# Retention and output projection of a hybrid RWKV and retention block: four raw value buffers, four split weight buffers, constants and gates loaded behind the first fourteen loads

## The chip, the core and the metric

The kernel runs on one core of one Trainium2 chip. The core has a matrix engine (PE, whose weight loads are listed apart as PEld), a vector engine (DVE), a scalar engine (ACT), a general engine (POOL) and an engine that issues most of the DMA transfers (SP). Each engine works through its own list of instructions in a fixed order; an instruction that waits for a semaphore holds up everything behind it on its engine, and a DMA that waits holds up the DMAs behind it in the queue of the engine that issues it. The metric is the device time of one execution in microseconds (us). Before the change, three runs gave 2503.66 to 2504.76 us, with a median of 2504.42 us.

## The reference

One layer mixes 1024 latent tokens, behind 256 context tokens, in two branches: a bidirectional RWKV scan, and a bidirectional retention with 4 heads, keys and queries 256 wide, values 512 wide, in chunks of 128 tokens. The change touches the retention and the pools that the output projections use. For one direction the retention is:

```
def step(S, inp):
    kc, vc = inp[0], inp[1]
    S_new = S * c_dec + jnp.einsum('bhck,bhcv->bhkv', kc * k_dec, vc)
    if not with_out:
        return S_new, None
    qc = inp[2]
    scores = jnp.einsum('bhik,bhjk->bhij', qc, kc) * intra
    o = (jnp.einsum('bhij,bhjv->bhiv', scores, vc)
         + jnp.einsum('bhik,bhkv->bhiv', qc * q_dec, S))
    return S_new, o
```

`intra`, `q_dec`, `k_dec` and `c_dec` are exponentials of a per-head decay times token distances. Forward and backward outputs are added, normalised per head, multiplied by a gate and projected. The RWKV branch ends in the same way. Both projections are merged by channel gates, and a last projection and an RMSNorm follow.

## The kernel before

**Arithmetic.** Large products are done in three passes: an operand is split into a rounded part `hi` (a cast on ACT, line 210) and a rest `lo` (a subtraction on DVE or POOL, line 211), and PE adds hi x hi, hi x lo and lo x hi. The helper is `split`.

**Stages.** Up to about 1795 us of the trace the kernel computes the input projections and the RWKV scans. Then `phase2` opens: `retention` runs the four heads, and `out_a` follows, which normalises the RWKV output (`rwkv_norm`) and multiplies it by the weights `wa` (products `ya`). The scheduler interleaves the two, so `ya` products run while the retention goes on. `phase3` does, for each half of 512 tokens, the retention's projection (weights `wr`, products `yr`, 8 blocks of 4 weight groups each), the merge with the channel gates, and the last projection (weights `wo`, products `po`, lines 1541 to 1556).

**One head** (`ret_head`). The state of the backward direction is built over the chunks 1, 0, 9, 8, down to 3. For each pair of chunks: `ret_load` brings the keys (tile `rs`, 256 KB), PE transposes them (`ktp`, line 1395), ACT scales them (`kx`, line 1399) and DVE computes the rest of the split (line 1400). For each chunk `ret_vals` brings the values (tile `vr`, 256 KB, line 1380) and splits them into `vt` (ACT line 210, POOL line 211; DVE for the very first two chunks). `ret_state` multiplies both (`st`, lines 1414 to 1416), and DVE adds the result to the decayed old state (line 1429). Then chunks 2 to 9 give outputs: scores `sc`, the states times the decayed queries (`ro`, line 1475, the queries scaled by POOL in line 1408), the scores times the values (into the same `ro`), and `ret_norm`: statistics, normalised tile `on`, the gate tile `gr` (loaded in line 1497), four transposes `ot`, ACT's scale and bias, POOL's product with `gr` (line 1506), and the store (line 1507). `ret_decay` makes the decays of a head from two constant tiles, `dist` (256 KB) and `io` (128 KB), that are loaded once, for head 0 (lines 1456 and 1457).

**Buffers.** A tile of a tag gets the next of that tag's buffers and waits until its last reader is done. Lines 41 and 42 set their numbers. `VR` counts the raw values (tag `vr`): a load into a `vr` buffer waits for the POOL subtraction of the value that held it. `VT` counts the split values, `RS` keys and queries. `WR` counts raw weights, and `WH` the tiles `hi` and `lo`, which `weights` uses for `wa`, `wr` and `wo`, and `rwkv_norm` for its sums. In `ya` and `yr` each split weight serves 12 matmuls in a row. In `po`, eight weights are used in two groups of four; within a group four token tiles each use all four weights, 48 matmuls in all, so that all four stay in use until the last tile of the group.

**Order.** A scheduler places the instructions on each engine. Two helpers tie it down: `lead` remembers an instruction under a letter, and `late` forbids an instruction to stand ahead of the one remembered. `load` (line 573) issues a DMA on SP that may not stand ahead of the lead "s". `first` (line 1354) makes each of the retention's first `FIRSTL` = 14 loads the lead "s" in turn; these are the keys and values of head 0 for the chunks 1, 0 and 9 to 3 (the last of them is the value of chunk 3). A plain `nc.sync.dma_start` is not tied in this way. In the DMA queues, each new transfer also waits until the transfer eight before it has landed.

Of the kernel before, what the change touches and what calls it, by code (L numbers as in the profile page):

```python
# [15 lines left out]
P = 128  # L16
# [21 lines left out]
XB = 14  # L38
EARLY = 6
LAG = 2  # L40
VR, VT, RS, KX, S1, S0, ON = 2, 11, 6, 3, 9, 2, 2
WR, WH, AR = 3, 5, 2
RES = 4
MUE = 1
VAE = 0
# [83 lines left out]
class Kern:  # L129
# [1303 lines left out]
    def ret_head(self, h, dist, io):  # L1433
        nc = self.nc
# [18 lines left out]
            if c > 2:  # L1453
                sb[c - 1] = self.ret_state(h, 1, k1, vt, c, sb[c])
        if h == 0:
            nc.sync.dma_start(dist.rearrange("p a b -> p (a b)"), self.ins["k_dist"])
            nc.sync.dma_start(io.rearrange("p a b -> p (a b)"), self.ins["k_iota"])
        qd, mk = self.ret_decay(h, dist, io)
        for c in range(2, 10):
            if c % 2 == 0:  # L1460
# [24 lines left out]
    def ret_norm(self, h, t0, po):  # L1485
        nc, pv = self.nc, self.pv
        on = self.rt("on", [P, 512], ON)
        st = self.rt("bst", [P, 6], 4)
        nc.vector.bn_stats(st, po)
        mv = self.rt("bmv", [P, 4], 4)  # L1490
        nc.vector.bn_aggr(mv[:, 0:2], st)
        nc.scalar.activation(mv[:, 2:3], mv[:, 1:2], AF.Ln, bias=self.eps[:, 2:3])
        nc.scalar.activation(mv[:, 2:3], mv[:, 2:3], AF.Exp, scale=-0.5)
        nc.vector.tensor_scalar(on, po, mv[:, 0:1], mv[:, 2:3], op0=ALU.subtract, op1=ALU.mult)
        yield
        gr = self.rt("gr", [P, 4, P], 2)
        nc.sync.dma_start(gr, self.grD[4 * h:4 * h + 4].rearrange("v p t -> p v t")[:, :, t0:t0 + P])
        pt = self.rpsum("ot", (P, 4, P))
        for v in range(4):
            nc.tensor.transpose(pt[:, v, :], on[:, P * v:P * v + P], self.ident)  # L1500
        y = on.rearrange("p (v t) -> p v t", v=4)
        for v in range(4):
            b = 4 * h + v
            nc.scalar.activation(y[:, v, :], pt[:, v, :], AF.Identity, scale=self.ph[:, PV_RLW + b:PV_RLW + b + 1],
                                 bias=self.ph[:, PV_RLB + b:PV_RLB + b + 1])
        nc.gpsimd.tensor_tensor(y, y, gr, op=ALU.mult)
        nc.sync.dma_start(self.orD[4 * h:4 * h + 4].rearrange("v p t -> p v t")[:, :, t0:t0 + P], y)
        yield
# [87 lines left out]
```

## Time and profile before

The profiled execution took 2498.37 us, of which the trace spans 2496.6 us; the runs' median of 2504.42 us is 6.05 us above it. In the table, the columns are windows of the trace (us), the busy time of PE, DVE and ACT within them, and the mean rate of the transfers.

| window | what runs | length | PE | DVE | ACT | GB/s |
|---|---|---|---|---|---|---|
| 0 to 1795 | input projections, RWKV | 1795.00 | 1722.90 | 1212.90 | 853.81 | 144 |
| 1795 to 2200 | retention, `ya` | 405.00 | 380.54 | 283.22 | 205.31 | 185 |
| 2200 to 2496.6 | rest of `yr`, merge, `po` | 296.60 | 282.54 | 153.10 | 102.97 | 173 |

The profile gives for each group of instructions the line, engine, operation and tiles, written out<-in. In timelines each row has its start, its duration, and in brackets the time for which its engine had been idle, with what ended the wait. "SPq" is SP's queue of DMAs. The granted clock (PEclk) is the share of TensorE's full speed that the throttle let through. PE fills 96% of the whole span.

### The profile page before, as it was taken

The numbers are of one execution on the slowest core, as the hardware profiler recorded it, in microseconds if no ns is written. First come the engines' busy times: TensorE is split into PE (matmuls) and PEld (weight loads), VectorE is DVE, ScalarE is ACT, GpSimd is POOL, SyncE is SP. The second block draws the span as 40 slices with busy tenths as digits, with TensorE's granted clock in tenths as the row PEclk, the third lists the DMA queues.
The fourth block names the chain that finished last, engine by engine and source line by source line (L and its number), as shares of the span: only waits on it lengthen the run. The fifth ranks groups of instructions, "written<-read, shape, count | busy, mean of one in ns | idle before, by whom it ended". The sixth has DMA issues, their size and how long they took to land.

```text
span 2496.6 us, 53437 instructions
## 1 busy us (share of the span) xinstructions
PE 2386.0 (96%) x21200; PEld 1926.1 (77%) x21200; DVE 1649.2 (66%) x2882; ACT 1162.1 (47%) x2547; POOL 562.3 (23%) x688
## 2 busy tenths in 40 slices
PE   7999999999999899997999999999898998999998
PEld 4888888777888899986777777777666765678786
DVE  5497897797796254434887787884378657754644
ACT  6434334334334334444655666554356435543422
POOL 2211021211021001211222322222276335400000
PEclk9999999999999899998999999999999999999999
DMA  6143344343344625354546556554465755585552
GB/s 250 50 149 118 140 152 135 133 141 121 135 156 152 199 88 146 106 139 124 157 145 175 163 170 192 149 160 135 123 187 165 224 160 156 180 285 170 182 174 85
DMA packets 335660, 385.07 MB, mean 154 GB/s; under 512 B 86954, under 2 KB 240306, under 8 KB 331314
## 3 DMA queue, kind: packets, MB, share of 16 engines
q1 hardware_dynamic: 304370, 298.80, 39.0%
q0 software_dynamic: 10944, 55.58, 6.7%
q10 hardware_dynamic: 20096, 27.27, 3.1%
q8 instruction: 167, 2.74, 0.4%
q14 instruction: 83, 0.68, 0.1%
HBM read 264.63 MB, written 116.92 MB: 153 GB/s over the span
## 4 chain that ended last, share of the span: by engine, by line
PE 53%; DMA 5%; DVE 5%; ACT 3%; issue 2%; SPq 2%; POOL 2%; ACTq 0%; DVEq 0%; POOLq 0%
PE gm L556 10%; PE gv L556 7%; PE ro L1475 3%; PE A L556 2%; PE yr L1276 2%; PE yr L1274 2%; PE yr L1275 2%; DMA bi<-bkD 2%; PE S L556 2%; PE X L556 2%; PE bt L1043 2%; PE gm L330 2%; PE gm L332 1%; PE gm L331 1%; PE U L556 1%
## 5 line engine op out<-in xcount | busy, mean ns | idle before, releaser
L330 PE MATMUL gm<-uh,wh 128*128 128x512 f32 x896 | 354.2, 396 | 16.2 <-ACT xp L402 13.7
L331 PE MATMUL gm<-ul,wh 128*128 128x512 f32 x896 | 353.7, 395 | 0.7 <-DVE ul L299 0.7
L332 PE MATMUL gm<-uh,wl 128*128 128x512 f32 x896 | 353.2, 394 | 0.0
L330 PEld LDWEIGHTS gm<-uh,wh 128*128 128x128 f32 x896 | 169.6, 190 | 51.5 <-ACT xp L402 15.0
L1063 POOL TENSOR_TENSOR sp<-sv,pc 64x256 f32<-64x256 f32 x152 | 104.9, 690 | 424.9 <-DVE sv L1087 202.3
L331 PEld LDWEIGHTS gm<-ul,wh 128*128 128x128 f32 x896 | 169.8, 189 | 38.4 <-DVE xnt L298 1.7
L332 PEld LDWEIGHTS gm<-uh,wl 128*128 128x128 f32 x896 | 169.7, 189 | 34.9
L556 PE MATMUL gm<-uh,wlo 128*128 128x512 f32 x416 | 171.0, 411 | 0.7 <-DVE wlo L658 0.7
L556 PE MATMUL gm<-ul,whi 128*128 128x512 f32 x416 | 171.3, 412 | 0.0
L556 PE MATMUL gm<-uh,whi 128*128 128x512 f32 x416 | 170.8, 411 | 0.0
L658 DVE TENSOR_TENSOR wlo<-wraw,whi 128x256 fp32r<-128x256 f32 x168 | 81.0, 496 | 122.5 <-ACT whi L657 121.3
L556 PE MATMUL gv<-whi,uh 128*128 128x256 f32 x512 | 148.7, 290 | 0.3 <-issue 0.3
L211 DVE TENSOR_TENSOR lo<-raw,hi 128x512 fp32r<-128x512 f32 x128 | 92.3, 726 | 85.2 <-ACT hi L210 85.0
L556 PE MATMUL gv<-whi,ul 128*128 128x256 f32 x512 | 147.7, 289 | 0.0
L556 PE MATMUL gv<-wlo,uh 128*128 128x256 f32 x512 | 147.6, 288 | 0.0
L210 ACT CAST hi<-raw 128x512 fp32r<-128x512 f32 x128 | 78.6, 620 | 140.1 <-PE yr L1275 74.1
L902 DVE TENSOR_TENSOR TL<-TL,tmp 128x31 f32<-128x31 f32 (+15 forms) x310 | 135.3, 436 | 8.5
L1077 ACT COPY uv<-U 64x256 f32<-64x256 f32 x160 | 58.6, 366 | 156.3 <-PE U L556 82.7
L900 DVE TENSOR_TENSOR tmp<-E,TL 128x31 f32<-128x31 f32 (+15 forms) x310 | 124.0, 400 | 8.9
L1087 DVE TENSOR_TENSOR sv<-S,sp 64x256 f32<-64x256 f32 x144 | 60.7, 422 | 103.1 <-PE S L556 58.6
L1475 PE MATMUL ro<-s,rs 128*128 128x512 f32 x256 | 123.7, 596 | 4.8 <-DVE s L1429 4.3
L210 ACT CAST wh<-wr 128x1024 fp32r<-128x1024 f32 x56 | 58.8, 1050 | 130.7 <-PE gm L331 127.2
(298 smaller groups left out, 6228.1 us busy)
## 6 DMA issues: line engine op xcount, KB each, us to landing
wr<-in_w_in SPq DMA_DIRECT2D x56, 512.0 KB, 3.5
wraw<-in_w_in SPq DMA_DIRECT2D x84, 256.0 KB, 3.6
bkD<-bk POOLq DMA_DIRECT2D x16, 1280.0 KB, 5.6
bk<-bkD SPq DMA_DIRECT2D x80, 256.0 KB, 3.6
krD<-kr POOLq DMA_DIRECT2D x16, 1024.0 KB, 4.4
raw<-in_wr SPq DMA_DIRECT2D x64, 256.0 KB, 3.1
vtD<-vt POOLq DMA_DIRECT2D x64, 160.0 KB, 3.9
bi<-bkD SPq DMA_DIRECT2D x160, 64.0 KB, 2.6
```

Of the source, the lines that this page charges most:

```text
L210: nc.scalar.copy(hi, src)
L211: (eng or nc.vector).tensor_tensor(lo, src, hi.bitcast(F32), op=ALU.subtract)
L330: nc.tensor.matmul(acc[:, :n], hi[:, k, :], self.hi(k, t0, n), start=(k == 0), stop=False)
L331: nc.tensor.matmul(acc[:, :n], hi[:, k, :], self.lo(k, t0, n), start=False, stop=False)
L332: nc.tensor.matmul(acc[:, :n], lo[:, k, :], self.hi(k, t0, n), start=False, stop=(k == KT - 1))
L556: return self.pin(self.nc.tensor.matmul(*a, **k))
L658: self.late(nc.vector.tensor_tensor(lo[:, j % size, k:k + 2], r, h.bitcast(F32), op=ALU.subtract), "v")
L900: self.late(nc.vector.tensor_tensor(t3, et[:, j + 1:, j:j + 1].broadcast_to([P, n, m]), tl[:, j:j + 1, 0:m].broadcast_to([P, n, m]), op=AL ...
L902: self.late(nc.vector.tensor_tensor(tl[:, j + 1:, 0:m], tl[:, j + 1:, 0:m], t3, op=ALU.subtract), "v")
L1063: nc.gpsimd.tensor_tensor(sp[ch], sv[ch, h], pcs[ch].broadcast_to([64, 4, C]), op=ALU.mult)
L1087: self.lead("v", nc.vector.tensor_tensor(new[h], ps[ch], sp[ch], op=ALU.add))
L1475: nc.tensor.matmul(po, qx[d][:, k, cols], st[:, k, :], start=(d == 1 and k == 0), stop=False)
```

## The change

Raw values get four buffers in place of two. Split weights get four in place of five, for `hi` and for `lo`. The memory that the one takes is what the other gives up: a `vr` buffer holds 2 KB in each partition, and so do a `hi` and a `lo` buffer. The constants `dist` and `io`, and the gate tiles `gr` of all heads (32 loads), are issued through `load`, and so stand behind the first fourteen loads. Nothing that is computed changes.

```
-VR, VT, RS, KX, S1, S0, ON = 2, 11, 6, 3, 9, 2, 2
-WR, WH, AR = 3, 5, 2
+VR, VT, RS, KX, S1, S0, ON = 4, 11, 6, 3, 9, 2, 2
+WR, WH, AR = 3, 4, 2
...
         if h == 0:
-            nc.sync.dma_start(dist.rearrange("p a b -> p (a b)"), self.ins["k_dist"])
-            nc.sync.dma_start(io.rearrange("p a b -> p (a b)"), self.ins["k_iota"])
+            self.load(dist.rearrange("p a b -> p (a b)"), self.ins["k_dist"])
+            self.load(io.rearrange("p a b -> p (a b)"), self.ins["k_iota"])
...
         gr = self.rt("gr", [P, 4, P], 2)
-        nc.sync.dma_start(gr, self.grD[4 * h:4 * h + 4].rearrange("v p t -> p v t")[:, :, t0:t0 + P])
+        self.load(gr, self.grD[4 * h:4 * h + 4].rearrange("v p t -> p v t")[:, :, t0:t0 + P])
```

Every engine's order up to the retention stays as it was. From there on the scheduler places things anew. SP's order at the start of head 0 (a minus marks a row of before, a plus a row of the change; a row without either stands in both). `vr_21720` and `vr_21725` are the values of chunks 9 and 8, `vr_21762` and `vr_21767` those of 7 and 6, `rs` are keys and queries:

```order
 L1386 DMA rs_21718<-kD 128x2x256
+L1380 DMA vr_21720<-vD 128x512
+L1380 DMA vr_21725<-vD 128x512
 L1386 DMA rs_21760<-kD 128x2x256
 L1386 DMA rs_21802<-kD 128x2x256
 L1386 DMA rs_21844<-kD 128x2x256
-L1456 DMA dist<-in_k_dist 128x512
-L1457 DMA io<-in_k_iota 128x256
-L1380 DMA vr_21720<-vD 128x512
+L1380 DMA vr_21762<-vD 128x512
 L1386 DMA rs_21886<-kD 128x2x256
 L1386 DMA rs_21888<-qD 128x2x256
```

The values of chunks 9 and 8 have moved ahead of the keys of the later chunks. The constants have left this place; they come, with the first gates, five value loads further on.

ACT's order at the same place. `vt_21722` and `vt_21727` are the split values of chunks 9 and 8, `vt_21764`, `vt_21769` and `vt_21806` those of 7, 6 and 5, `s` are copies of first states, and `kx_21735` is the scaling of the keys of chunks 9 and 8:

```order
+L210 CAST vt_21722<-vr_21720 128x512
+L210 CAST vt_21727<-vr_21725 128x512
 L1427 COPY s_2775_21674<-st_21675 128x512
 L1427 COPY s_2775_21674<-st_21680 128x512
-L210 CAST vt_21722<-vr_21720 128x512
+L210 CAST vt_21764<-vr_21762 128x512
 L1427 COPY s_2781_21696<-st_21697 128x512
 L1427 COPY s_2781_21696<-st_21702 128x512
-L210 CAST vt_21727<-vr_21725 128x512
+L210 CAST vt_21769<-vr_21767 128x512
+L210 CAST vt_21806<-vr_21804 128x512
 L1399 ACTIVATE kx_21735<-ktp_21730,ph 128x512
```

Two casts stood ahead of the first of these key scalings, and now five do. The rows that follow on ACT go up to the key scalings of chunks 7 and 6 (`kx_21777`) and of 5 and 4 (`kx_21819`); `vt_22301` and `vt_22306` are the first two values of head 1:

```order
-L210 CAST vt_21764<-vr_21762 128x512
-L210 CAST vt_21769<-vr_21767 128x512
+L210 CAST vt_21811<-vr_21809 128x512
+L210 CAST vt_21848<-vr_21846 128x512
 L1399 ACTIVATE kx_21777<-ktp_21772,ph 128x512
-L210 CAST vt_21806<-vr_21804 128x512
-L210 CAST vt_21811<-vr_21809 128x512
+L210 CAST vt_21853<-vr_21851 128x512
+L210 CAST hi_24336<-ar_24333 128x512
+L210 CAST vt_22301<-vr_22299 128x512
+L210 CAST vt_22306<-vr_22304 128x512
 L1399 ACTIVATE kx_21819<-ktp_21814,ph 128x512
```

The casts of values run three to five chunks further ahead of the key scalings than before.

ACT's order in the first of the last projections (first half of the tokens). `hi_26420` is the fifth weight of `wo`, `hi_26429`, `hi_26438` and `hi_26447` are the sixth to eighth, and the `act` tiles are activations of the second half, loaded ahead. Before, `hi_26420` stood six rows ahead of `act_26815`; now it reads:

```order
 L210 CAST act_26810<-ar_26808 128x512
 L210 CAST act_26815<-ar_26813 128x512
+L210 CAST hi_26420<-raw_26419 128x512
 L210 CAST hi_26429<-raw_26428 128x512
 L210 CAST hi_26438<-raw_26437 128x512
-L210 CAST hi_26447<-raw_26446 128x512
 L210 CAST act_26820<-ar_26818 128x512
 L210 CAST act_26825<-ar_26823 128x512
+L210 CAST hi_26447<-raw_26446 128x512
```

The fifth weight's cast has moved behind the activation `act_26815`, next to the sixth, and the eighth's behind two further activations.

## The prediction, made before the change was run

> **What bounds the kernel now.** I begin with the head of the page.
>
> ```profile
> span 2496.6 us, 53437 instructions
> PE 2386.0 (96%) x21200; PEld 1926.1 (77%) x21200; DVE 1649.2 (66%) x2882; ACT 1162.1 (47%) x2547; POOL 562.3 (23%) x688
> ```
>
> PE is busy for 96% of the span, so only PE's gaps, and matmuls at a low clock, can be won. Next come the windows over the stages from the start of the retention to the end. The columns are: window, its length, then busy us and instructions of PE, PEld, DVE, ACT and POOL, the granted clock, the DMA share, GB/s.
>
> ```profile
> 1802.50:1808.60 6.10, 0.01 (x1) 0.01 (x1) 1.43 (x3) 2.79 (x5) 1.83 (x2) 0.78 0.90 287
> 1808.60:1826.20 17.60, 15.34 (x65) 11.66 (x65) 12.22 (x19) 8.68 (x16) 12.42 (x11) 0.88 0.62 203
> 1826.20:1882.00 55.80, 54.88 (x212) 33.70 (x212) 44.29 (x74) 33.44 (x81) 41.19 (x33) 1.00 0.62 185
> 1882.00:1912.00 30.00, 23.37 (x108) 17.63 (x109) 26.77 (x39) 17.28 (x35) 18.63 (x16) 1.00 0.44 144
> 1912.00:2080.00 168.00, 168.00 (x744) 114.74 (x743) 106.25 (x180) 73.65 (x177) 76.57 (x59) 1.00 0.61 190
> 2080.00:2120.00 40.00, 32.63 (x135) 22.41 (x134) 32.63 (x53) 22.41 (x47) 19.21 (x17) 0.96 0.45 139
> 2306.30:2352.00 45.70, 43.16 (x189) 35.07 (x188) 28.07 (x57) 21.19 (x53) 0.00 (x0) 1.00 0.50 162
> ```
>
> Where products with the output weights fill the gaps (1912 to 2080) PE has no idle time at all. What is idle lies in four places: the start of head 0 (6.09 us, then 2.26), heads 1 and 3 while they build states (6.63 and 7.37), and the first output projection (2.54). In heads 1 and 3 DVE is busy for 26.77 of 30.00 us (89%) and 32.63 of 40.00 (82%), so values that arrive earlier meet a busy DVE there. Only at the start of head 0 is it a load that PE waits for. The timelines of PE and of ACT (start, us, instruction, in brackets the idle time before it and what ended it):
>
> ```profile
> 1801.61 0.66 PE L1395 MATMUL ktp<-ident,rs 128*128 128x128 f32 x4
> 1808.59 0.79 PE L1414 MATMUL st<-vt,kx 128*128 128x512 f32 x1 [6.33 <-ACT kx L1399]
> 1809.18 0.63 PE L1415 MATMUL st<-vt,kx 128*128 128x512 f32 x1
> 1809.61 0.63 PE L1414 MATMUL st<-vt,kx 128*128 128x512 f32 x1
> 1818.33 0.50 PE L1414 MATMUL st<-vt,kx 128*128 128x512 f32 x1 [0.78 <-ACT kx L1399]
> 1826.16 1.10 PE L1475 MATMUL ro<-s,rs 128*128 128x512 f32 x2 [1.48 <-DVE s L1429]
> ```
> ```profile
> 1804.25 0.62 ACT L210 CAST vt<-vr 128x512 fp32r<-128x512 f32 x1 [4.44 <-DMA vr<-vD]
> ...
> 1807.34 0.62 ACT L210 CAST vt<-vr 128x512 fp32r<-128x512 f32 x1 [1.50 <-DMA vr<-vD]
> 1807.86 0.68 ACT L1399 ACTIVATE kx<-ktp,ph 128x512 fp32r<-128x512 f32 x1
> ```
>
> The matmul at 1808.59 waits for scaled keys, whose inputs were there at 1802.3. The scaling stood in ACT's order behind two casts of values, and the second cast waited for its load. SP issued those loads so:
>
> ```profile
> 1799.49 0.34 SPq L1456 DMA_DIRECT2D dist<-in_k_dist  x1
> 1799.87 0.54 SPq L1457 DMA_DIRECT2D io<-in_k_iota  x1
> 1800.52 0.38 SPq L1380 DMA_DIRECT2D vr<-vD  x1
> 1800.93 0.52 SPq L1386 DMA_DIRECT2D rs<-kD  x1
> 1801.56 0.56 SPq L1386 DMA_DIRECT2D rs<-qD  x1
> 1802.21 0.54 SPq L1380 DMA_DIRECT2D vr<-vD  x1
> 1802.81 0.97 SPq L1497 DMA_DIRECT2D gr<-grD  x2
> 1806.29 10.24 SPq L1380 DMA_DIRECT2D vr<-vD  x5
> ```
>
> **The front of head 0.** SP stood still before 1799.49; the first row of the next fence (what SP's queue waited for, total, times, longest) says for what. In the new order the values of chunks 9 and 8 stand ahead of that wait and have buffers of their own, so both are in the chip before 1799; the 6.33 us as they are now would go. But ACT's order changes too: the key scaling for chunk 9 now stands behind five casts, of chunks 9, 8, 7, 6 and 5. So what is late next is the load of chunk 5. Behind the wait SP now issues key, key, chunk 7, key, query, chunk 6, chunk 5: at 0.34 to 0.56 us each the seventh goes out at about 1799.49 + 6 x 0.5 = 1802.5. It ends 7 x 256 KB = 1.79 MB of transfers. Before, 1.41 MB (dist, half as much for io, chunk 9, key, query, chunk 8) had landed at 1807.34. At the 287 GB/s of the first window the further 0.38 MB take 1.3 us, which gives 1808.6; by time in flight (chunk 8: 1802.21 to 1807.31, 5.1 us by its rows on issue and cast) it is 1802.5 + 5.1 = 1807.6. I take 1808.1 + 0.52 for the cast + 0.68 for the scaling + 0.05 = 1809.4 for the first matmul, **0.8 us later** than 1808.59. The bounds: if that load flew as briefly as the shortest of its kind (2.6 us, below) it would land at 1805.1 and PE start at 1806.4, 2.2 us earlier; if the seven loads moved at the 203 GB/s of the second window, it would land at 1799.49 + 8.8 + 2.6 = 1810.9, PE start at 1812.2, 3.6 us later.
>
> ```profile
> SPq L1456 <- DMA mbD<-gp: 10.7, 1, 10.7
> SPq L573 <- POOL ar L1316: 71.2, 32, 6.9
> SPq L1380 <- POOL vt L211: 32.2, 22, 3.0
> DMA to landing us min/median/max: 2.6/3.9/6.2
> L211 POOL TENSOR_TENSOR vt<-vr,vt x38: 1262/1293/1744, 1805.0 to 2084.4; 128x512 fp32r<-128x512 f32 x38
> ```
>
> After the long gap PE runs slow: its starts lie 0.43 us apart (1809.18 to 1809.61) at a granted clock of 0.78 and 0.88 in the first two windows, against 0.226 on average where PE is full (168.00 us for 744 matmuls from 1912 on). This stays if the gap stays. The Trainium skill, "TensorE: Matmul & The Clock Gate", Part 1, says that an idle window of about 3.4 us halves PE's clock until it has been busy about as long again. The 0.43 us agree with the halving. By that rule a gap shortened under 3.4 us would also win back the slow stretch, and I use it only for the rival below.
>
> Behind 1808.59 the pace was one value for every trip of load, cast and POOL subtraction (1.29 us median), because two raw buffers went round. With four, that pace goes. Another head-of-line wait could come in its place: the scaling for chunks 5 and 4 now stands behind the casts of head 1's first two values. The later of their loads needs the buffer of chunk 4, whose subtraction ends at about 1809.4 + 0.5 + 1.29 = 1811.2; with a median flight of 3.9 us and 1.25 us for cast and scaling the keys are ready at 1816.4. PE wants them when it wanted them before and waited (1818.33 - 0.78), plus the 0.8: at 1818.4. Cover 2.0 us, just under the longest flight's excess (2.3). So what is late next there is PE's own work (15.34 of 17.60 us), then DVE's sums (12.22). Of its idle time 0.78 is waiting behind casts, and 1.48 at the first output is DVE's. I let the first go and keep the second. So the front gives +0.8 - 0.8 = **0.0**, from -3.0 (2.2 earlier and the 0.78) to +3.6.
>
> **Constants and gates.** These move behind the first 14 loads: dist and io (384 KB), and all 32 gr loads. The first reader of dist and io ahead of the outputs is the decay for the queries, whose output is wanted by POOL 12 us after PE's start (below at 1822.10). The new place in SP's order is behind the load of chunk 3, which waits for the POOL subtraction of chunk 7; by the pace of the old rows this is around 1810, and with the longest flight (6.2 us) both are there by 1817. Cover: 5 us. If it failed, first output and every later one would move by the overrun, one to one, since POOL then starts its 2.54 us late.
>
> ```profile
> 1822.10 2.54 POOL L1408 TENSOR_TENSOR rs<-rs,qd 128x512 f32<-128x512 f32 x2
> ```
>
> The first two gr loads were issued at 1802.81 and are read after the first output at 1826.16 has been normalised. They go out one and two value loads behind the constants, by about 1812; with the longest flight they are there at 1818, 8 us ahead of 1826.16. I cost them at 0.
>
> **Heads 1 to 3.** All later values run through four buffers, so the 32.2 us in which SP waited for POOL's value subtractions shrink, while the 71.2 us of waits for the RWKV norm's buffers stay; SP's order is one line, so part of the first returns in the second. In heads 1 and 3 the amount of DVE work between the first key scaling and the first score is the same but for one or two instructions, and DVE filled 89% and 82% there. Value: **0**. Ends: if a third of the idle 14.0 us went, -4.7; if the new order costs each of the two stages one more stall as long as its longest (1.76 us, next row), +3.5.
>
> ```profile
> 1890.55 0.50 PE L1414 MATMUL st<-vt,kx 128*128 128x512 f32 x1 [1.76 <-ACT kx L1399]
> ```
>
> **Four split weights.** In the yr and ya products a weight lasts for 12 matmuls, 12 x 0.23 = 2.8 us, so three weights ahead are 8.3 us of cover: nothing. In the last projection (po) four weights are used together by four token tiles, 48 matmuls. With five buffers the fifth weight is split before they begin to come free; with four it must wait for the first. At the first projection this reads:
>
> ```profile
> 2309.10 0.62 ACT L210 CAST hi<-raw 128x512 fp32r<-128x512 f32 x1
> ...
> 2320.65 0.62 ACT L210 CAST act<-ar 128x512 fp32r<-128x512 f32 x1 [2.16 <-DMA ar<-orD]
> 2321.18 1.66 ACT L210 CAST hi<-raw 128x512 fp32r<-128x512 f32 x3
> 2321.91 1.89 DVE L211 TENSOR_TENSOR lo<-raw,hi 128x512 fp32r<-128x512 f32 x3
> 2321.84 1.19 PE L1550 MATMUL po<-hi,mg 128*128 128x512 f32 x4 [1.73 <-ACT hi L210]
> 2335.20 1.20 PE L1550 MATMUL po<-hi,mg 128*128 128x512 f32 x4 [0.81 <-ACT hi L210]
> ```
>
> The three casts at 2321.18 are of the sixth to eighth weight; the fifth had been cast at 2309.10, and its 12 matmuls lay between. In the new order the fifth weight's cast has moved behind the activation cast that ran at 2320.65, ahead of the sixth. So it can't begin before 2321.18 unless that activation's load comes sooner, and PE, which used to spend 12 x 0.227 = 2.7 us on it (45.17 us for 199 matmuls in the last projection, its row below) before the stall, now stalls first: 1.73 becomes 4.4, and the other weights' stalls are covered by the displaced work. Term: **+2.7**. It would be 0 if that load came 2.7 us sooner, and with the clock drop that followed the 6.33 us gap (0.2 us for each of some ten matmuls) it would be 2.7 + 2 = 4.7. The second change of weights (2335.20) I keep at 0.81. In the second half, at 2465 and later, no activations are cast any more. There the first weight is free 9 matmuls, 2.05 us, before the group changes; a cast of 0.52 and a subtraction of 0.63 (the rows above, by three) fit in: 0.
>
> **Sum.** 0.0 + 0 + 0 + 2.7 = +2.7 us on the execution in the trace, 2498.37 -> 2501.1. The median of the runs shown is 2504.42, 6.05 above this execution, so I forecast **2507.1 us**.
>
> **Rivals.**
> (a) *The queue is freed.* The five casts don't hold the keys, since all seven loads come at the shortest flight, and heads 1 and 3 lose a third of their stalls: -3.0 - 4.7 + 2.7 = -5.0; with the gap under the point where the clock falls (about eight matmuls at 0.43 instead of 0.23, -1.6) and the projection's stall unchanged, -9.3, 2495.1. For it: SP's 32.2 us of waits on POOL, and a load that ends the one long gap. Against: ACT's order, and the busy DVE. The Trainium skill, "Perfetto Trace Analysis", section Optimization Strategy, says that gaps which repeat "can mean there isn't enough SBUF/PSUM for the next tile to be allocated". By it four buffers help all four heads; the trace bears this out only for SP's waits, as PE's repeated gaps are ended by key scaling and not by the casts of values. Chance 0.25.
> (b) *The weights' pool becomes the bound.* Each change of four weights in po stalls PE, not only the first: there are seven behind the first group (two halves, two column blocks, two groups in each, less one). Price: a cast and a subtraction after release, 1.15 us, plus an ACT or DVE job in the way, about 0.6: 1.8 each, or 7 x 1.8 = 12.6 -> 2517.0. It decides where ACT gets to the cast over 0.9 us (2.05 - 1.15) after the release. For it: the gap at 2335.20, already ended by a cast. Against: PE is busy 45.17 of 45.20 us in the last projection. Likelier is a half of it, two to four stalls. Chance 0.2.
> (c) *Nothing moves.* The loads' waits are replaced by waits one step on, and the projection's activation load comes sooner by what SP saved: 2504.4. Chance 0.15.
>
> ```profile
> 2440.00:2485.20 45.20, 45.17 (x199) 36.99 (x198) 20.17 (x50) 14.25 (x42) 0.00 (x0) 1.00 0.20 59
> ```
>
> **How the numbers follow.** The forecast with its terms near zero gets 0.4. A measurement of this kernel tells about 0.2%, 5 us, from no change: 2499.4 to 2509.4. Of the forecast's 0.4, 0.28 lies within that, 0.10 above, 0.02 below; (a) gives 0.21 faster and 0.04 same; (b) 0.15 slower, 0.05 same; (c) 0.13 same, 0.02 faster. Sums: faster 0.25, same 0.50, slower 0.25. The range: the forecast's own ends are -3.0 - 4.7 + 0 = -7.7 and 3.6 + 3.5 + 4.7 = +11.8; all at one end together is unlikely, so I go from rival (a)'s -9.3 to +9.1, which leaves out half of (b), 0.1, and about 0.05 on each side of the rest: 2495 to 2513.5.
>
> **What would show it.** PE's first state matmul behind the four transposes at 1801.6: 1809 (forecast) or under 1806.4 (rival a). What ended its wait: the scaling of keys on ACT, behind a cast that a value's load ended. SP's waits for POOL's value subtractions: well under 32 us. First output matmul: 1826 +- 1. In the first projection one stall of 4 us or more in place of 1.73. In the second half PE 45.1 of 45.2 us busy, or gaps of a microsecond at each group for (b). The forecast is wrong if chunk 5's load lands before 1805 or after 1811, if a head's state stage changes its idle time by over 4 us, or if the activation load at 2320 moves.

## The result, and the profile after

The changed kernel took 2517.95 us (median of six runs, 2512.06 to 2521.24), the kernel before 2504.04 us beside it. The ratio is 1.0055, with a 95% interval of 1.0036 to 1.0074: **slower by 0.55%**, where no difference was forecast. The head of the page of the changed kernel:

```profile
span 2516.5 us, 53412 instructions
PE 2397.8 (95%) x21200; PEld 1930.3 (77%) x21200; DVE 1650.0 (66%) x2882; ACT 1161.2 (46%) x2547; POOL 562.1 (22%) x688
```

The work of DVE, ACT and POOL is the same to a microsecond; PE is busy 11.8 us longer with the same 21200 matmuls, and idle for longer too (118.7 us against 110.6). The two spans differ by 19.9 us, more than the medians do. Part of it has nothing to do with the change: every engine's order is the same up to the retention, and yet the first state matmul stands at 1795.9 us in the one trace and at 1802.5 in the other. So below I count from there. **D** is the time from the start of the first state matmul of the retention to the start of the last matmul of the last projection. Groups of instructions by form, with the shortest, median and longest duration in ns and the first and the last start, of the kernel before and of the changed one:

```profile
L1414 PE MATMUL st<-vt,kx x144: 387/397/799, 1795.9 to 2167.6; 128*128 128x512 f32 x144
L1552 PE MATMUL po<-hi,mg x128: 388/389/389, 2306.8 to 2484.8; 128*128 128x512 f32 x128
```
```profile
L1414 PE MATMUL st<-vt,kx x144: 387/397/799, 1802.5 to 2179.6; 128*128 128x512 f32 x144
L1552 PE MATMUL po<-hi,mg x128: 388/389/628, 2323.7 to 2505.0; 128*128 128x512 f32 x128
```

D is 688.8 us before and 702.5 after (more digits than the rows show are from the records). The difference of 13.7 us is close to that of the medians, 13.9. Each kernel was profiled a second time (e9 and e10 below): D = 691.4 and 704.7. Windows over D, two profiles of the kernel before, then two of the changed one (columns as in the prediction):

```profile
1795.90:2485.20 689.30, 663.08 (x2844) 490.13 (x2844) 427.80 (x736) 305.18 (x676) 204.22 (x158) 0.99 0.56 180
```
```profile
1800.80:2492.50 691.70, 668.79 (x2844) 494.60 (x2844) 427.36 (x736) 304.78 (x676) 203.81 (x158) 0.98 0.55 179
```
```profile
1802.50:2505.40 702.90, 670.98 (x2844) 492.11 (x2844) 428.24 (x735) 303.12 (x676) 203.77 (x158) 0.99 0.56 176
```
```profile
1802.30:2507.40 705.10, 676.29 (x2844) 496.89 (x2844) 429.58 (x735) 302.71 (x676) 203.35 (x158) 0.98 0.55 176
```

On the means, the length grows by 13.5 us: PE's idle time by 5.8 (24.6 to 30.4), its busy time by 7.7 for the same 2844 matmuls. Where these are follows stage by stage.

**The front of head 0**: PE, ACT and SP of the changed kernel.

```profile
1817.33 0.79 PE L1414 MATMUL st<-vt,kx 128*128 128x512 f32 x1 [7.06 <-ACT kx L1399]
1826.91 0.50 PE L1414 MATMUL st<-vt,kx 128*128 128x512 f32 x1 [0.73 <-ACT kx L1399]
1834.76 1.10 PE L1475 MATMUL ro<-s,rs 128*128 128x512 f32 x2 [1.18 <-DVE s L1429]
```
```profile
1805.26 1.14 ACT L210 CAST vt<-vr 128x512 fp32r<-128x512 f32 x2
1806.51 1.07 ACT L1427 COPY s<-st 128x512 f32<-128x512 f32 x2
1811.96 0.62 ACT L210 CAST vt<-vr 128x512 fp32r<-128x512 f32 x1 [4.38 <-DMA vr<-vD]
...
1815.43 1.25 ACT L210 CAST vt<-vr 128x512 fp32r<-128x512 f32 x2 [1.89 <-DMA vr<-vD]
1816.59 0.68 ACT L1399 ACTIVATE kx<-ktp,ph 128x512 fp32r<-128x512 f32 x1
```
```profile
1816.07 0.62 ACT L210 CAST vt<-vr 128x512 fp32r<-128x512 f32 x1
```
```profile
1809.61 4.65 SPq L1380 DMA_DIRECT2D vr<-vD  x4
```

The casts of chunks 9 and 8 run at 1805.26 without a wait: their values came early, as the change has it. But the key scaling stands behind three more casts, of chunks 7, 6 and 5, and starts at 1816.59. Chunk 6's load ended the wait of 1.89 us; chunk 5's cast, the second of that row and shown again by itself, followed at 1816.07, as soon as its own load had landed. PE waits 7.06 us in place of 6.33, with the split values for twelve state matmuls lying ready.

**The gate matmuls.** These are 64 records of line 784, a vector times matrix product with one output row in each of four groups of columns. The windows of these instructions alone, then PE's pieces in time, before and after:

```profile
2020.00:2100.00 80.00, 5.93 (x64) 1.43 (x64) 1.67 (x4) 0.98 0.65 197
```
```profile
2020.00:2100.00 80.00, 9.81 (x64) 1.72 (x64) 1.67 (x4) 1.00 0.55 164
```
```profile
2025.67 1.03 PE L784 MATMUL gacc<-raw,gsil 128*1 128x256 f32 x12
2051.43 0.60 PE L784 MATMUL gacc<-raw,gsil 128*1 128x256 f32 x6
```
```profile
2068.71 0.59 PE L784 MATMUL gacc<-raw,gsil 128*1 128x256 f32 x2
2072.05 0.59 PE L784 MATMUL gacc<-raw,gsil 128*1 128x256 f32 x2
2074.07 0.60 PE L784 MATMUL gacc<-raw,gsil 128*1 128x256 f32 x4
2075.66 0.59 PE L784 MATMUL gacc<-raw,gsil 128*1 128x256 f32 x2
```

A piece of two records takes 0.59 us, one of six 0.60, one of twelve 1.03. Before, the scheduler put them in 7 pieces; now they lie in 15, and PE is busy with them for 3.9 us more, in a stage in which it has next to no idle time (181.80 of 182.00 us busy from 1921 to 2103). The ends of matmuls are modelled in the profile; from the start of each piece to the start of the matmul behind it, which needs no modelled end, the pieces add up to 5.4 and 9.0 us, 3.6 more. The expectations below count in this way.

**Heads 1 and 3, and the end of the other branch's products**, changed kernel:

```profile
1890.28 0.50 PE L1414 MATMUL st<-vt,kx 128*128 128x512 f32 x1 [1.80 <-ACT kx L1399]
1895.34 0.50 PE L217 MATMUL mu<-hi,ones 128*128 128x512 f32 x1 [1.34 <-ACT hi L210]
1919.76 1.10 PE L1475 MATMUL ro<-s,rs 128*128 128x512 f32 x2 [1.66 <-DVE s L1429]
2105.74 0.50 PE L217 MATMUL mu<-hi,ones 128*128 128x512 f32 x1 [1.54 <-ACT hi L210]
2117.05 0.51 PE L217 MATMUL mu<-hi,ones 128*128 128x512 f32 x1 [1.34 <-ACT hi L210]
2221.93 0.47 PE L1274 MATMUL ya<-act,hi 128*128 128x512 f32 x1 [1.48 <-DVE ma L1291]
```

Norm matmuls (`mu`) stand in PE's order ahead of the time when their operands are ready. Before, they waited for 3.9 us in all, the longest for a subtraction on POOL; now it is 4.6 us, the longest for casts on ACT. And 1.48 us of waiting are new where the last `ya` products want an accumulator that DVE has not emptied. All waits of over 0.05 us between the first output and the first `yr` product add up to 17.6 us (16.3 in the second profile), against 14.9 (14.0).

**The first projection**, ACT and PE of the changed kernel:

```profile
2337.67 0.62 ACT L210 CAST act<-ar 128x512 fp32r<-128x512 f32 x1 [1.75 <-DMA ar<-orD]
2338.19 1.65 ACT L210 CAST hi<-raw 128x512 fp32r<-128x512 f32 x3
```
```profile
2338.86 1.86 PE L1550 MATMUL po<-hi,mg 128*128 128x512 f32 x4 [4.57 <-ACT hi L210]
2340.52 0.63 PE L1551 MATMUL po<-lo,mg 128*128 128x512 f32 x1
2340.94 0.63 PE L1552 MATMUL po<-hi,mg 128*128 128x512 f32 x1
```

One wait of 4.57 us stands in place of 1.73 and 0.81, and the starts behind it lie 0.42 us apart where they were 0.227: the clock has fallen. The stage from its first to its last matmul takes 49.8 us, against 46.5.

### The profile page after: what moved, and what is told of

It is laid out like the page before. It is cut to its first block, busy times and chain, and to the rows that moved or that the text cites. A ratio compares the mean times of both kernels' runs of the same rounds, so it can differ in the third digit from the quotient of the medians.

```text
span 2516.5 us, 53412 instructions
## 1 busy us (share of the span) xinstructions
PE 2397.8 (95%) x21200; PEld 1930.3 (77%) x21200; DVE 1650.0 (66%) x2882; ACT 1161.2 (46%) x2547; POOL 562.1 (22%) x688
## 5 line engine op out<-in xcount | busy, mean ns | idle before, releaser
L330 PE MATMUL gm<-uh,wh 128*128 128x512 f32 x896 | 353.8, 396 | 16.2 <-ACT xp L402 13.7
L1429 DVE SCALAR_TENSOR_TENSOR s<-s,ph,st 128x512 f32<-128x512 f32 x128 | 90.7, 739 | 42.6 <-PE st L1416 36.1
```

Source lines behind the costliest of these rows:

```text
L330: nc.tensor.matmul(acc[:, :n], hi[:, k, :], self.hi(k, t0, n), start=(k == 0), stop=False)
L1429: nc.vector.scalar_tensor_tensor(new[:, k], old[:, k], self.cd[:, d, h:h + 1], a, op0=ALU.mult, op1=ALU.add)
```

## The experiments

The theory: **three costs** that have little to do with one another, the wait at the fifth weight (from the weight buffers), the gate matmuls in pieces, and the waits of the retention (both from the order that the scheduler makes of the rest); and in the front, casts that stand ahead of the key scaling. Rivals: the weight buffers do it all; the moved loads do it all; the single execution was unlucky. Ratios are to the kernel before; the wait is all of PE's idle time in the first projection.

| run | gate pieces | D, us | that wait, us | median, us | ratio (95%) |
|---|---|---|---|---|---|
| before | 7 | 688.8; 691.4 | 2.5; 1.8 | 2504.04 | |
| whole change | 15 | 702.5; 704.7 | 4.6; 3.9 | 2517.95 | 1.0055 (1.0036 to 1.0074) |
| e1: four weight buffers alone | 7 | 694.4 | 4.5 | 2507.70 | 1.0025 (1.0014 to 1.0036) |
| e2: moved loads alone | 12 | 695.1 | 1.7 | 2507.40 | 1.0021 (1.0008 to 1.0035) |
| e3: change without moved loads | 8 | 697.5 | 4.3 | 2510.15 | 1.0027 (1.0016 to 1.0038) |
| e4: change, own weight buffers in po | 15 | 698.9 | 0 | 2513.36 | 1.0048 (1.0029 to 1.0066) |
| e5: change, casts held in head 0 | 7 | 690.7 | 4.0 | 2499.77 | 0.9992 (0.9978 to 1.0005) |
| e6: e4 and e5 | 7 | 687.0 | 0 | 2499.87 | 0.9992 (0.9980 to 1.0004) |
| e7: e6 without moved loads | 15 | 701.8 | 0 | 2512.14 | 1.0032 (1.0017 to 1.0047) |
| e8: before, gate order forced | 12 | 695.7 | 1.8 | 2506.06 | 1.0021 (1.0005 to 1.0038) |
| e11: change, gate priority | 9 | 699.1 | 3.8 | 2516.45 | 1.0067 (1.0045 to 1.0089) |
| e12: before, constants moved | 7 | 690.8 | 2.1 | 2500.88 | 0.9994 (0.9982 to 1.0005) |
| e13: before, gate tiles moved | 7 | 688.9 | 2.2 | 2497.67 | 0.9982 (0.9965 to 0.9998) |
| e14: e6, casts held in all heads | 8 | 690.5 | 0 | 2504.36 | 1.0007 (0.9995 to 1.0020) |
| e15: e6, gate tiles as before | 7 | 687.8 | 0 | 2496.95 | 0.9979 (0.9963 to 0.9995) |

Each ratio goes with executions of the kernel before that ran beside that run: their medians were 2502.25 us for e1 to e4, 2500.78 for e5 to e8, 2500.93 for e11 and e12, and 2500.32 for e13 to e15. The ratios come from all executions and differ from the quotients of these medians by up to 0.0013.

### One part of the change at a time

The edits of e1, e2 and e3 are lines of the diff, or leave lines of it out.

```
e1  -WR, WH, AR = 3, 5, 2
    +WR, WH, AR = 3, 4, 2
e2  dist, io and gr through self.load, VR = 2, WH = 5
e3  VR = 4, WH = 4, dist, io and gr through nc.sync.dma_start
```

> Only the split weights go from five buffers to four; all else is the kernel before. D is the time in the trace from the first state matmul of the retention to the last matmul of the last projection: 688.8 us before, 702.5 with the whole change. Theory of three costs (the first output projection +3.3, the gate matmuls cut into more pieces +3.4, the rest in the retention): the stall at the fifth weight is 4.6 us in place of 1.73 + 0.81, with slow matmuls behind it, D = 692; the gate matmuls stay in 7 pieces at 5.4 us. Rival, the weight buffers are all of it (they also stall the RWKV projection and the norms): D = 700 to 703. Time: 2507 against 2516.

> Only dist, io and the gate tiles go behind the first fourteen loads; two value buffers, five weight buffers. Theory of three costs: the gate matmuls of line 784 stand in 12 pieces in place of 7, at 0.42 us for a piece +2.1; the first values leave one microsecond earlier since the constants don't stand ahead, -1; the projection keeps its 1.73 + 0.81: D = 690. Rival, the moved loads are the main cost: D = 698 or more. Rival, nothing: D = 688.8.

> The whole change without the moved loads (four value buffers, four weight buffers). Theory of three costs: gate matmuls in 8 pieces (+0.4), the projection's stall of 4.6 us (+3.3), the key scaling of chunk 9 behind four casts of values, a first wait of 6 to 8 us: D = 692.5 to 695. Rival, the weight buffers are all of it: D = 700 to 703. Rival, the moved loads are all of it: D = 689.

The weight buffers alone cost 5.5 us against the runs beside them (2502.25), the moved loads alone 5.2, the change without the moved loads 7.9 (by the ratios 6.3, 5.3 and 6.8): neither rival that names one edit holds. The value buffers, the first edit of the change, have no run of their own. e3 and e1 differ in them alone, and the intervals of the two overlap almost wholly, so beside four weight buffers they show no cost in time. In e1 the wait at the fifth weight came as expected:

```profile
2329.42 2.08 PE L1550 MATMUL po<-hi,mg 128*128 128x512 f32 x4 [4.46 <-ACT hi L210]
```

Its D is 2.4 us above the 692 expected: 0.97 us of waiting at the first `yr` product, and 20.5 us at a granted clock of a half, against 10.2. In e2, whose D is 5.1 us above the 690 expected, the retention itself ended 5.5 us sooner (its last output matmul at 374.7 us of D, against 380.2). All of that was given back at the end of the `ya` products, where DVE had to empty an accumulator behind a subtraction that waited for a weight's cast, and that for its load. PE, ACT and DVE of e2:

```profile
2213.96 0.77 PE L1274 MATMUL ya<-act,hi 128*128 128x512 f32 x1 [7.19 <-DVE ma L1291]
```
```profile
2211.22 0.62 ACT L210 CAST hi<-raw 128x512 fp32r<-128x512 f32 x1 [5.16 <-DMA raw<-in_wa]
```
```profile
2211.87 0.69 DVE L211 TENSOR_TENSOR lo<-raw,hi 128x512 fp32r<-128x512 f32 x1 [5.09 <-ACT hi L210]
...
2213.13 0.68 DVE L1291 SCALAR_TENSOR_TENSOR ma<-ma,ya 128x512 f32<-128x512 f32 x1
```

I had expected neither of these waits. e3 has a longer one at the first `yr` product (3.76 us, ended by a weight's cast on ACT), and its D is 2.5 us above the upper end of what was expected.

### The wait in the projection

```
-                        w[k] = self.weights(ins["wo"][:, k:k + 1, cols])
+                        raw, whi, wlo = [tile([P, 1, 512], "wo" + tag, bufs, dt) for tag, dt, bufs in
+                                         (("r", F32, WR), ("h", F32R, 8), ("l", F32R, 8))]
+                        self.load(raw, ins["wo"][:, k:k + 1, cols])
+                        self.split(whi, wlo, raw)
+                        w[k] = (whi, wlo)
```

> The whole change, but the weights of the last projection have buffers of their own, eight of each kind; up to the projections every engine's order is that of the whole change. Theory of three costs: the 4.57 us stall and the 1.3 us of slow matmuls behind it go, D = 702.5 - 5.9 = 696.6, and the stalls in the retention stay (7 us at its start). Rival, the stall only moves to the next weight or to a load: D = 700 or more.

The first projection of e4, window from its first to its last matmul:

```profile
2317.80:2362.20 44.40, 44.40 (x193) 35.99 (x191) 29.88 (x66) 21.77 (x56) 0.00 (x0) 1.00 0.50 168
```

PE is full for all 44.40 us, 5.4 less than in the changed kernel. So this cost is the buffers' and stands by itself. D fell by 3.6 to 698.9 only, 2.3 short of the expectation. One reason is a wait of 2.39 us at the first `yr` product, where the changed kernel had 0.40. The other is that the repair has a cost of its own, to be seen in the second half of the last projection, in which no kernel waits. The same window there, in e4 and in the changed kernel:

```profile
2450.90:2495.30 44.40, 44.40 (x192) 35.99 (x191) 19.66 (x51) 12.12 (x41) 0.00 (x0) 1.00 0.13 42
```
```profile
2461.70:2505.00 43.30, 43.30 (x192) 35.84 (x191) 20.11 (x47) 14.34 (x41) 0.00 (x0) 1.00 0.22 65
```

With eight buffers the matmuls of the last projection follow one another at 232 ns in place of 227, in all five runs that have them, which is 1.1 us for each half. No run shows why.

### The front

```
-        self.split(vt[c][:, 0], vt[c][:, 1], raw, self.nc.gpsimd if h or c > 1 else None)
+        cast = self.nc.scalar.copy(vt[c][:, 0], raw)
+        if h == 0 and 1 < c < 8:
+            self.late(cast, "k")
+        (self.nc.gpsimd if h or c > 1 else self.nc.vector).tensor_tensor(vt[c][:, 1], raw, vt[c][:, 0].bitcast(F32), op=ALU.subtract)
```

> The whole change, and in head 0 the cast of each value from chunk 7 on may not stand ahead of the key scaling of the pair before it, so that the first scaling stands behind the casts of its own chunks 9 and 8 alone. If the first wait (7.06 us) comes from ACT's order, the scaling runs as soon as its transposes are there: wait under 1 us, no slow stretch behind it (-3.4), though up to 3 us of waiting for the values of chunks 7 and 6 may follow: first output at 23 to 27 us from the first state matmul in place of 32.3. Besides, the gate matmuls are back in 7 pieces in this order (-3.5). D = 688 to 693 in place of 702.5. If it comes from the loads, the first output stays at 30 or later, D = 697 to 702.

PE of e5 (the edit moves its line numbers by three; line 1417 is line 1414 of before):

```profile
1809.04 0.50 PE L1417 MATMUL st<-vt,kx 128*128 128x512 f32 x1 [0.78 <-ACT kx L1402]
1815.65 0.79 PE L1417 MATMUL st<-vt,kx 128*128 128x512 f32 x1 [3.13 <-ACT kx L1402]
```

The wait of 7.06 us came from ACT's order: held back, the casts let the scaling through after 0.78 us. Some of the time returns at the next pair of chunks, 3.13 us with a slow stretch behind it, and the first output stands at 28.9 us of D, less of a gain than the 23 to 27 expected. D fell by 11.8 us all the same, for behind head 0 too the order is another one, with the gate matmuls in 7 pieces. Of the 11.8 us, 3.4 lie ahead of the first output, where the casts were held; 7.4 lie between it and the first `yr` product, 3.9 of them in the gate matmuls; 1.1 lie behind. With this one constraint the whole loss is gone, with the buffers and the loads of the change left in place (2499.77 us, ratio 0.9992), but only the 3.4 us stand where it forbids anything. The rest came with the order of the later heads that the scheduler made of it, and that was luck: e7 below has the same constraint and the other order.

> Both repairs: casts of values held behind the key scalings in head 0, and buffers of their own, eight of each kind, for the last projection's weights. If the costs are separate they add up: D = 702.5 - 7 to -10 (front) - 3.5 (gate matmuls in 7 pieces) - 5.9 (no stall and no slow matmuls in the first projection) = 683 to 688, under the 688.8 of the kernel before: about 2501 us, ratio 0.998 to 1.000. If a new wait takes their place: D = 692 or more.

> As the run with both repairs, but dist, io and the gate tiles are issued as before the change. In this order the gate matmuls of line 784 stand in 15 pieces again, not in 7. If cutting them costs what the sums of steps say, they take 9 us in place of 5.4 and D is 3 to 4 us above the run with both repairs; the front is up to 1 us later since the constants are loaded earlier. If the pieces cost nothing, D is within 1.5 us of it.

Both repairs together give D = 687.0, as expected if they add up; in time they can't be told from the kernel before. e7 was to test the gate matmuls by themselves and doesn't: its D is 14.7 us higher, not 3 to 4, since its whole order behind head 0 is like that of the changed kernel (its third head's last product of states and queries at 296.6 us of D, the changed kernel's at 296.8, e6's at 288.9). It shows that leaving the loads where they were can bring the bad order as well, and that neither repair keeps it away.

### The gate matmuls

```
e8   -            for q in range(4):
     +            for q in (2, 3, 0, 1):
     ...
     +                self.late(mm, "g")
     ...
     +                self.lead("g", mm)
e11  +            with self.tc.high_priority(offset=URGENT):
                      for q in range(4):
```

In e8 each of these matmuls is held behind the one emitted before it.

> The kernel before, with one edit: the four gate matmuls of a step are kept in the order third, fourth, first, second, by which the scheduler cuts them into 12 pieces in place of 7; up to there every order is that of before. If pieces cost PE time: their steps add up to 6.5 to 7.7 us in place of 5.4, D = 690 to 691. If only the place in the order matters and not the cutting: 5.4 us, D = 688.8.

> The whole change, with the gate matmuls of line 784 given a high priority in the scheduler, which leaves 9 pieces in place of 15; up to 20 PE rows ahead of the first of them PE's order is that of the whole change. If pieces cost PE time, their steps add up to 6 to 6.7 us in place of 9.0 and D falls by 2.5 to 3, to 699.5 to 700. If the cost lies in waiting for their weights, D stays at 702 or more.

The windows of the gate matmuls alone, e8 and then e11:

```profile
2020.00:2100.00 80.00, 7.24 (x64) 1.16 (x64) 1.67 (x4) 1.00 0.64 200
```
```profile
2020.00:2100.00 80.00, 7.36 (x64) 1.49 (x64) 1.68 (x4) 1.00 0.63 197
```

In 12 pieces they are busy for 7.24 us against 5.93 in 7; in 9 pieces for 7.36 against 9.81 in 15. So cutting costs PE time, with its size set by how the cuts fall. (In steps from start to start this is 6.4 and 7.4; e8 just missed its bound of 6.5, and e11 missed 6 to 6.7.) D doesn't follow cleanly: e8 rose by 4 to 7 us, to 695.7 where 690 to 691 was expected, with 2.88 us of new waiting at the `yr` products, and e11's fall of 3.4 isn't seen in its median (2516.45). Their share in the time of the whole change is read from the trace, and no run shows it alone.

### Once more, and the moved loads apart

> The kernel before, profiled once more, to see how far D (first state matmul of the retention to the last matmul of the projection) and the time at a low clock within it vary for one program. If D belongs to the order of the instructions: 688.8 +- 2. If it is a matter of the single execution: 683 to 695.

> The whole change, profiled once more. If D and the gate matmuls' sum belong to the order: D = 702.5 +- 2, 9.0 us in 15 pieces, a stall of 4.4 to 4.7 us in the first projection. If it was one unlucky execution: 692 to 698.

D moved by 2.6 us for the kernel before and by 2.2 for the changed one, a little outside the 2 expected, with 13.3 to 13.7 between them: it belongs to the order, not to the execution. In e10 the gate matmuls came as expected (9.0 us in 15 pieces), and the stall in the projection fell short, with 3.95 us where 4.4 to 4.7 was expected.

> The kernel before, with dist and io alone behind the first fourteen loads; the gate tiles as before. Gate matmuls in 7 pieces. If it takes both moves together to change the order of the heads that follow (64 lines of difference on PE here, against 479 from this kernel to the one with both): D = 688 to 690, the first wait one microsecond shorter (5.3). If the constants alone cost what both cost: D = 694 to 696.

> The kernel before, with the gate tiles alone behind the first fourteen loads; dist and io as before. Both moves together cost 5.2 us (2507.4 against 2502.25), the constants alone nothing. If the gate tiles alone carry it: D = 694 to 696 and about 2506 us. If it takes both, since only both together change the order of the later heads (65 lines of difference on PE here, 479 between the two and the constants alone): D = 688 to 692 and no difference in time.

Alone, the constants change nothing (0.9994), and the gate tiles gain a little, 0.18% (interval 0.02 to 0.35%). Both together lose 0.21%. In the trace of e2 no engine waits for over 0.15 us for the constants or for a gate tile. So it isn't that the moved loads come too late; the pair of moves makes the scheduler lay out the later heads anew.

> As the run with both repairs, but casts of values from chunk 7 on are held behind the key scalings in all four heads. If casts that stand ahead of a key scaling also cause the waits of heads 1 and 3 (13.0 us in the retention behind the first output in the run with both repairs), these fall to 8 to 10 us and D to 682 to 684. If those waits have another cause (DVE, the norms of the other branch), D = 686 to 690. Gate matmuls in 8 pieces.

> As the run with both repairs, with dist and io behind the fourteen loads but the gate tiles issued as before. Gate matmuls in 7 pieces. If the costs follow from the order, and this order has 7 pieces, no stall in the projection and the short first wait: D = 685 to 689, as the run with both repairs (687.0). If the gate tiles' place matters by itself: D = 692 or more.

Holding the casts back in all heads doesn't lower the waits behind the first output (15.3 us, against 13.0 in e6; D = 690.5), so that theory falls: casts ahead of key scalings aren't what heads 1 and 3 wait for. e15, with the constants moved, the gate tiles where they were, and both repairs, came as expected at D = 687.8, and with 0.9979 (0.9963 to 0.9995) is faster than both kernels, if by little.

## Why the prediction was wrong

**The size and the sign.** Forecast was 2507.1 us, in a range of 2495 to 2513.5; it is 2517.95. The forecast was +2.7 us, the medians differ by 13.9.

**The step that failed** stands at its start: "only PE's gaps, and matmuls at a low clock, can be won". By this PE's own work was a constant, and the sum has terms for waits alone. The profiles show 7.7 us more of busy time for the same matmuls, 3.9 of them in the gate matmuls that were cut into more pieces, and 5.8 us more of waiting, of which the 2.1 in the projection had been forecast. Even the sum of all its upper ends, +11.8, lies below 13.9. None of the signs that its last sentence names for being wrong appears: on the time scale of the trace before, chunk 5's load landed at 1809.5, inside 1805 to 1811; the idle time of the two state stages went from 6.63 and 7.37 us to 8.15 and 7.83; and the activation's cast in the projection starts 14.45 us behind the stage's first matmul, where it was 14.31.

Term by term:

- *The front, 0.0.* The order was read rightly: the last thing that the key scaling waits for is the load of chunk 5. It let its cast start at 1816.07; less the 6.5 us by which the trace is late, the load landed at 1809.5, with 1808.1 forecast (in the second pair of profiles it was 0.6 us later than forecast). PE's first matmul behind the scaling came 2.2 and 1.4 us later than before, with 0.8 forecast. PE's wait grew by 0.73 us in the first pair of profiles and by 1.40 in the second (4.82 to 6.22); in the first pair it grew by less than the delay because the state matmuls ahead of it ran at the low clock, which there only the changed kernel had. The gain of 0.78 behind it didn't come (0.73 was still waited). The first output is 2.1 and 1.2 us late: a small miss.
- *Constants and gates, 0.* **This step failed.** It asked whether the data would still be there in time, and they were. It didn't ask what else the scheduler moves when 34 loads are ordered in another way. e2 shows 5.2 us for it, e12 and e13 that neither part has a cost of its own. What the moved loads are worth inside the whole change isn't shown, as the order without them is another one too (e3, e7).
- *Heads 1 to 3, 0.* **This step failed most.** Its upper end, +3.5, covers the waiting and not the work. It compared the count of DVE's instructions in the two state stages and took equal counts for equal time. Behind the first output, PE's idle time grew by 2.5 us on the mean of two profiles each, and the gate matmuls, which the comparison of orders would have shown in 15 pieces in place of 7, by 3.9 us of busy time. I looked for differences where PE waits, and not at what PE does where it is full.
- *Four split weights, +2.7.* Right in place and cause: the fifth weight's cast ran behind the activation's (2337.67, then 2338.19), and the wait was 4.57 us with 4.4 forecast. The 0.81 that I kept vanished, as the cast behind had more time; the slow matmuls that I had put in the upper bound came. The stage grew by 3.3 us, and by 2.9 in the second pair (47.1 to 50.0).
- *Rival (b)*, a wait at every change of weights: refuted. In the second half no wait of over 0.05 us stands in any run. *Rival (a)*, a freed queue: it failed at the place named against it, ACT's order, and e5 shows what stood behind that.
- *The clock.* Of the 7.7 us of busy time 3.9 are the gate matmuls'. The other 3.8 are the same matmuls at the low clock: over D the granted clock stood at a half for 10.2 and 23.9 us before, and for 17.1 and 34.1 after. By that, 8.5 us more at a half cost an estimated 4.3, near the 3.8. But the two profiles of one program differ by 13.7 and 17.0 us in it, more than the means do, so two profiles don't show that this share is the change's. The runs as a whole point the same way: over the six of the changed kernel the granted clock is 0.9838 on the mean, over the 27 of the kernel before beside e1 to e4 it is 0.9861. The forecast put this term at nothing ("This stays if the gap stays"); it is the least sure of all.

By the means, then: 0.7 of waiting in the front, 2.5 in heads 1 to 3 and at the last `ya` products, 0.5 at the first `yr` products, 2.1 in the projection, 3.9 gate matmuls in pieces, 3.8 slower matmuls. Together 13.5 us. What stays open is why the scheduler falls from one order of the later heads into the other; the runs show that it does, and that no single edit carries it.

The rule that was weighed as a rival, from the Trainium skill, "Perfetto Trace Analysis", section Optimization Strategy, by which gaps can mean too few buffers, is not borne out here: with twice the buffers for raw values the long gap grew from 6.33 to 7.06 us, and it shrank to 0.78 when ACT's order was held.

## What to carry to other kernels

Where a scheduler orders the work, more buffers let it run loads and casts further ahead, and an in-order engine may then put them in front of the one small instruction that the bound engine waits for; holding the casts back took the first wait from 7.06 us to 0.78, where twice the buffers had lengthened it. What such a constraint does to the rest of the order is a matter of chance: with it the ratio was 0.9992 in e5 and 1.0032 in e7. When comparing two orders, look also at what the bound engine does in the stages in which it is full (how short matmuls that overlap are cut up), and not only at its waits. And a change that reorders half a stage should be judged by single edits and by their sums, for two that cost nothing alone cost 5 us together.

## What the runs showed of the hardware

One-row matmuls that go to different groups of columns overlap if they stand side by side: in the records up to four of them start 7 ns apart, and two, four or six took 0.59 to 0.60 us as one piece, twelve 1.03. And the clock fell to a half behind waits of well under 3 us in some profiles and not in others of the same program: in the second profile of the kernel before behind the wait of 1.96 us at the first state matmul, while the same wait in its first profile had no slow matmuls behind it. The Trainium skill, "TensorE: Matmul & The Clock Gate", Part 1, puts the fall behind an idle window of about 3.4 us. The wait of 4.57 us agrees with it, as the steps of 0.42 us behind it show. The waits of 1.5 to 2 us that were followed by slow matmuls don't: the window below is of the changed kernel, behind the 1.54 us at 2105.74.

```profile
2107.00:2110.40 3.40, 3.40 (x10) 2.54 (x9) 2.95 (x5) 2.00 (x4) 2.59 (x3) 0.50 0.31 92
```

PE is full and the granted clock is 0.50. Here the measurement decides: what a short wait costs can't be read from its length alone.

The record shows what else counts. In each of the 17 profiles all stretches at half clock begin at whole multiples of 3.413 us from one another, as if the clock were set on a grid. Of the grid's steps at full clock, from 7 us ahead of D to its end, 70 were followed by a step at half clock; in these PE was idle for 1.5 to 3.4 us. In the 3353 others it was idle for at most 1.9. So about half a step of idle time was enough, in one wait or in several, and a wait that a step's border divides counts for less. The wait of 1.96 us shows both; the rows are two steps each, of the second and of the first profile of the kernel before (columns as above):

```profile
1797.46:1800.87 3.41, 1.46 (x9) 0.99 (x9) 1.01 (x4) 2.06 (x5) 2.18 (x4) 1.00 0.47 98
1800.87:1804.28 3.41, 3.41 (x9) 2.63 (x10) 1.98 (x3) 2.53 (x4) 0.00 (x0) 0.50 0.95 275
```
```profile
1792.30:1795.71 3.41, 1.69 (x10) 1.18 (x8) 1.01 (x4) 1.72 (x4) 2.17 (x4) 1.00 0.39 77
1795.71:1799.12 3.41, 3.18 (x14) 2.65 (x15) 2.33 (x4) 3.06 (x5) 0.00 (x0) 1.00 0.96 290
```

In the second profile the wait lies whole in one step, and the next runs at 0.50. In the first it is divided into 1.72 and 0.23 us, and the clock stays at 1.00. Where the grid lies differs between executions, so the same order meets it by chance.
